# Weight splits with a priority ahead of the other work of ScalarE and VectorE, in a hybrid decoder trunk

## The chip, the core and the metric

The kernel runs on one core of a Trainium2 chip. The core has five engines that work side by side and synchronise through semaphores: TensorE (PE in the profile, its weight loads PEld), VectorE (DVE), ScalarE (ACT), GpSimd (POOL) and SyncE (SP), which here only issues DMAs. The time is the device time of one execution in microseconds (us), lower being better. Three runs of the kernel before took 806.59, 806.67 and 807.04 us; the median is 806.67.

## What is computed

Two layers of a decoder trunk on 256 tokens of width 1024, in float32. In each layer a single input projection of the normalised stream feeds three mixers; each is gated, projected, merged by a sigmoid gate, and the sum goes through one output projection into the residual:

```python
for layer in range(DEPTH):                     # 2
    h = rms_norm(x, norm_w[layer])
    proj = jnp.einsum('bsd,de->bse', h, w_in[layer])     # 1024 -> 12832
    (a_xbc, a_z, a_dt, b_q, b_k, b_v, b_z,
     c_q, c_k, c_v, c_f, c_z, gates) = jnp.split(proj, split_at, axis=-1)
    y_a = mamba2_branch(a_xbc, a_z, a_dt, ...)           # convolution, chunked scan, group norm
    y_b = sliding_window_branch(b_q, b_k, b_v, b_z, ...) # rotary, 16 heads on 4 key heads, sinks
    y_c = forgetting_attention_branch(c_q, c_k, c_v, c_f, c_z, ...)  # 16 heads, decaying bias
    ys = jnp.stack([y_a, y_b, y_c], axis=2)
    branch = jnp.einsum('bsiw,iwd->bsid', ys, w_proj[layer])
    g = jax.nn.sigmoid(gates.reshape(b, s, N_BRANCH, d) + gate_bias[layer])
    merged = jnp.sum(g * branch, axis=2)
    x = x + jnp.einsum('bsd,de->bse', merged, w_out[layer])
return rms_norm(x, final_norm_w)
```

## The kernel before

**Three products for one.** The large products keep float32 accuracy with a faster number format, fp32r. Each operand is split into a high part, which is its copy in fp32r, and a low part, which is what the copy leaves over. A product is then high by high, plus low by high, plus high by low. `split` (lines 287 to 295) makes the two parts: one copy on ACT (line 290) and one subtraction on DVE (line 291), which needs the copy. It is used for the weights, which pass through it while the kernel runs, and for a few activations.

**Weights as a stream.** All weight matrices are cut into parts of 128 rows by 1024 numbers per partition (mostly four blocks of 256 columns or two of 512), in the order in which the products use them. `load_part` (line 351 on) issues a part's DMA on SP's queue into one of 6 `raw` buffers. `feed` (lines 383 to 396) takes the next part, allocates one of 6 `hi` and one of 6 `lo` buffers, and issues its split; then it has the next parts loaded, up to 6 ahead. `feed` is called by `release` (line 403) as soon as the matmuls that use a part for the last time have been written down, so at most 4 parts (`AHEAD`) are held by the program at that point; the buffers allow 6. Key and query weights (`turned`) are split in two halves with their columns rearranged.

**Work on PE.** PE's order is the order of the program text: the last two blocks stand in `tc.manual_schedule` for PE. `ops` lists the products, each a function such as `u_conv`, `u_cq`, `u_gate` or `u_proj`. Most of them accumulate one bank of PSUM (tag `mm`, 3 banks, rotated) over 8 blocks of 128 rows. After each product `pump` lets other work of PE in, in small doses: the generators `swa_quad`, `fox_quad`, `ssd_group` and others yield estimated waiting times (the `D_...` constants), and `pump` resumes one when its time is due on an estimated clock of PE. These use the tag `mx`, 5 banks. A product is emptied from its bank by ACT (lines 486 and 487 for the sums that GpSimd's queue then adds by an accumulating DMA, line 488; line 478 with line 479 on DVE where DVE adds them).

**Softmax chains.** `attn_quad` handles four heads: PE computes the scores, DVE subtracts a mask or bias and finds the maximum (L615, L623 to L628 for the sliding window, L646 for the forgetting attention), ACT takes the exponential and its sum (L610 or L652), DVE normalises (L635 to L639 with one small step on ACT, or L655 to L658), PE transposes the result (L113) and multiplies it by the values. There are 4 such quads of each kind in a layer.

**Order on ACT and DVE.** Only the opening is ordered by hand on all engines (the block at line 1425). For the rest a scheduler fixes each engine's queue at compile time: it walks through an estimated execution, and where several instructions of an engine could start, it takes the one that stands earliest in the program text. `tc.high_priority()` places the instructions traced inside it ahead of that order. Before the change it stands around the evictions of the first branch's projection (line 1015), the last branch's merge (line 1144) with the transposes and split behind it (line 1151), the layer's last additions and its norm (line 1204), and the split of the normalised stream of the next layer (line 1254). `pin` (line 284) does the opposite: it keeps an instruction behind what its engine has been given before; the splits of the last weights ahead of the output projection are pinned (`limit`, line 398), and appear in the profile under line 285, the wrapper's.

Of the kernel before, what the change touches and what calls it, by code (L numbers as in the profile page):

```python
# [16 lines left out]
P = 128  # L17
# [33 lines left out]
def hybrid_trunk(  # L51
# [17 lines left out]
    def T(tag, shape, dtype=F32, bufs=None):  # L69
        count[0] += 1  # L70
        return sb.tile(shape, dtype, tag=tag, name=f"{tag}_{count[0]}",
                       bufs=bufs if bufs is not None else BUFS.get(tag, 1))
# [8 lines left out]
    def pmx():  # L81
        return PS("mx", 5)
# [204 lines left out]
    def split(hi, lo, src, scale=None, keep=lambda f: f):  # L287

        if scale is None:
            keep(act)(hi, src, AF.Copy)  # L290
            keep(tt)(lo, src, hi.bitcast(F32), op=ALU.subtract)  # L291
        else:
            keep(act)(hi, src, AF.Copy, scale=scale)
            keep(stt)(lo, src, scale, hi.bitcast(F32), op0=ALU.mult, op1=ALU.subtract)
# [37 lines left out]
    turned = set()  # L332
    subs = []
    ops = []
    stream = []
    state = {"load": 0, "split": 0, "held": 0, "limit": None, "pin": False}
# [27 lines left out]
    def load_to(n_):  # L364

        while state["load"] < min(n_, len(stream)):
            load_part(state["load"])
            state["load"] += 1

    def new_part():  # L370

        j = state["split"]
        i, k = stream[j]
        n = subs[i][1]
        w = pieces.setdefault(i, Piece(n))
        load_to(j + 1)
        hi, lo = (T(tag, [P, min(NK - k, w.kper), n], F32R) for tag in ("hi", "lo"))
        state["held"] += 1
        w.parts.append((hi, lo))
        state["split"] += 1  # L380
        return raws.pop(j), hi, lo

    def feed(i=-1):

        lim = state["limit"]
        while state["split"] < len(stream) and state["split"] != lim and (
                state["held"] < AHEAD or stream[state["split"]][0] <= i):
            raw, hi, lo = new_part()
            keep = pin if state["pin"] else lambda f: f
            if stream[state["split"] - 1][0] in turned:  # L390
                for c in range(2):
                    split(*(v[:, :, c * P:(c + 1) * P].rearrange("p k (h e) -> p k h e", h=4) for v in (hi, lo)),
                          raw.rearrange("p k (h c e) -> p c k h e", h=4, c=2)[:, c, :, :, :], keep=keep)
            else:
                split(hi, lo, raw, keep=keep)
            load_to(state["split"] + N_RAW)

    def limit(j, keep):

        state["limit"], state["pin"] = j, keep  # L400
        feed()

    def release(w, n):
        if n > w.released:
            state["held"] -= n - w.released
            w.released = n
            feed()

    def run_op(i, f, last):
        if i is None:  # L410
            f()
            return
        feed(i)
        w = pieces[i]
        w.last = last
        f(w)
        if last:
            release(w, len(w.parts))
# [852 lines left out]
    for y in layers:  # L1271
# [11 lines left out]
        def cols(c0, n=256):  # L1283
            return sub([(0, w[:, c0:c0 + n])], n)
# [39 lines left out]
        if l == 0:  # L1324
            v, cv0, cv1 = cols(C_BV), cols(C_CV), cols(C_CV + 256)
# [8 lines left out]
        else:  # L1334
            cv0, v = cols(C_CV, 512), cols(C_BV)
# [89 lines left out]
    with tc.manual_schedule(engines={ENG.PE, ENG.DVE, ENG.Activation, ENG.Pool}):  # L1425
# [11 lines left out]
        p = pmx()  # L1437
# [98 lines left out]
        v = T("sm", [P, 8])  # L1536
# [55 lines left out]
```

## Time and profile before

| | us |
|---|---|
| median of 3 runs | 806.67 |
| the profiled execution's own time | 806.9 |
| its span, first to last instruction | 805.1 |
| PE busy, over 5160 matmul records | 796.5 |
| DVE busy | 684.2 |
| ACT busy | 533.8 |
| GpSimd busy | 167.5 |
| DMA, mean over the span | 212 GB/s |

A line of the profile names source line, engine, operation and tiles (written `out<-in`), the shapes, how often it was seen, the busy time in us and the mean of one in ns; then how long the engine had been idle before such instructions and what ended the idle time. In a timeline a row is the start in us, the duration in us, the engine, the line and the tiles; several instructions in a row of the same kind are merged (`x3`), and the engine's idle time before them stands in brackets with what ended it. A list of waits has total, count and longest wait. PE's matmuls are pipelined and their ends modelled, so their starts say more than their ends.

### The profile page before, as it was taken

To read this page: it belongs to the slowest core of one execution; us is meant where nothing else is said; L and a number is where in the kernel's file an instruction comes from. 1 tells how busy PE (TensorE), PEld (TensorE's weight loads), DVE (VectorE), ACT (ScalarE), POOL (GpSimd) and SP (SyncE) were. 2 spreads that over 40 slices of the span, in tenths; PEclk is the share of its full clock that TensorE was granted. 3 is DMA by queue.
4 is the path that set the end of the run, shared out by engine and by line. 5 is a ranking of instruction groups with operands and counts; after the bars stand their busy time and mean duration, and the time that the engine had idled before them with its cause. 6 is when DMAs were issued, how large, how long until landed. Compare 5 with 4: busy or idle time off the path is not lost.

```text
span 805.1 us, 14840 instructions
## 1 busy us (share of the span) xinstructions
PE 796.5 (99%) x5160; PEld 711.6 (88%) x5160; DVE 684.2 (85%) x1416; ACT 533.8 (66%) x1146; POOL 167.5 (21%) x236
## 2 busy tenths in 40 slices
PE   9999999999999999999999999999999999999996
PEld 8998988888998988888998899888889989888896
DVE  6878999997998997795785799999889999969865
ACT  7776768875775885543665678687657768755452
POOL 3166213140210100033001741122311220002000
PEclk9999999999999999999999999999999999999999
DMA  9997987797765565686678987679976546576632
GB/s 316 280 259 172 253 219 200 219 290 220 198 184 167 174 187 170 219 253 205 217 251 257 239 210 217 157 217 287 285 211 196 183 143 202 156 248 210 209 106 78
DMA packets 138827, 170.43 MB, mean 212 GB/s; under 512 B 9353, under 2 KB 106465, under 8 KB 138753
## 3 DMA queue, kind: packets, MB, share of 16 engines
q1 hardware_dynamic: 114960, 140.53, 55.5%
q0 software_dynamic: 13328, 13.29, 10.3%
q10 hardware_dynamic: 10464, 15.67, 6.7%
q8 instruction: 41, 0.67, 0.3%
q14 instruction: 34, 0.27, 0.1%
HBM read 154.71 MB, written 2.16 MB: 195 GB/s over the span
## 4 chain that ended last, share of the span: by engine, by line
PE 91%; issue 3%; DMA 2%; POOL 2%; DVE 1%; ACT 1%; POOLq 0%; DVEq 0%
PE mm L109 78%; PE mx L109 9%; PE mx L113 4%; DMA L<-L 1%; DMA hb<-in_sinks_dram 1%; POOL L L488 1%; DMA L<-in_x_dram 0%; DVE L L551 0%; ACT pp L610 0%; POOL L L285 0%; POOL L L562 0%; DVE lo L291 0%; POOL sm L224 0%; POOL L L571 0%; POOL L L572 0%
## 5 line engine op out<-in xcount | busy, mean ns | idle before, releaser
L109 PE MATMUL mm<-L,hi 128*128 128x512 f32 x1056 | 354.7, 387 | 0.5 <-ACT L L487 0.3
L291 DVE TENSOR_TENSOR lo<-raw,hi 128x1024 fp32r<-128x1024 f32 (+1 forms) x276 | 313.3, 1154 | 40.9 <-ACT hi L290 36.1
L109 PE MATMUL mm<-hi,L 128*128 128x512 f32 (+2 forms) x1168 | 303.1, 349 | 0.1
L290 ACT ACTIVATE hi<-raw 128x1024 fp32r<-128x1024 f32 (+1 forms) x276 | 265.6, 982 | 50.6 <-PE mm L109 30.0
L109 PE MATMUL mm<-L,lo 128*128 128x256 f32 x1056 | 266.6, 273 | 0.0
L109 PEld LDWEIGHTS mm<-hi,L 128*128 128x128 f32 x1168 | 205.8, 190 | 23.2 <-issue 1.5
L109 PEld LDWEIGHTS mm<-L,hi 128*128 128x128 f32 x1056 | 195.1, 190 | 27.4 <-issue 3.0
L109 PEld LDWEIGHTS mm<-L,lo 128*128 128x128 f32 x1056 | 202.1, 191 | 5.3
L109 PE MATMUL mm<-lo,L 128*128 128x512 f32 (+2 forms) x584 | 201.5, 347 | 0.0
L109 PEld LDWEIGHTS mm<-lo,L 128*128 128x128 f32 x584 | 110.2, 190 | 10.7
L488 POOL DMA_DIRECT2D L<-L x68 | 60.7, 915 | 192.5 <-ACT L L487 155.2
L1074 POOL TENSOR_SCALAR_AFFINE_SELECT bias<-bias 128x128 f32<-128x128 f32 x64 | 30.8, 513 | 82.7 <-DMA bias<-cumd 82.7
L829 DVE SCALAR_TENSOR_TENSOR L<-L,vec,L 128x255 f32<-128x255 f32 (+2 forms) x96 | 46.2, 481 | 1.9 <-ACT L L826 0.4
L486 ACT ACTIVATE L<-mm 128x256 f32<-128x256 f32 x84 | 31.9, 380 | 20.0 <-PE mm L109 14.0
L652 ACT ACTIVATE pp<-pp,nm 128x128 f32<-128x128 f32 x64 | 28.2, 443 | 22.8 <-DVE nm L646 22.8
L1109 ACT ACTIVATE L<-L 128x512 f32<-128x512 f32 x24 | 15.1, 631 | 34.5 <-DVE L L1106 30.8
L610 ACT ACTIVATE pp<-pp,nm 128x128 f32<-128x128 f32 x32 | 12.6, 394 | 24.9 <-DVE nm L615 24.1
L488 POOL DMA_DIRECT2D qt<-L x16 | 14.2, 925 | 71.4 <-ACT qt L487 64.6
L1142 POOL TENSOR_TENSOR L<-L,L 128x512 f32<-128x512 f32 x8 | 12.0, 1494 | 74.0 <-DVE L L1141 74.0
L487 ACT ACTIVATE L<-mm 128x256 f32<-128x256 f32 x68 | 26.2, 386 | 1.5 <-DMA L<-L 1.5
L1106 DVE TENSOR_TENSOR L<-mm,L 128x512 f32<-128x512 f32 x22 | 15.1, 687 | 11.2 <-PE mm L109 11.2
L551 DVE TENSOR_TENSOR L<-L,cs 128x256 f32<-128x256 f32 x40 | 20.0, 536 | 4.6 <-DMA L<-L 4.6
(213 smaller groups left out, 913.7 us busy)
## 6 DMA issues: line engine op xcount, KB each, us to landing
raw<-in_w_in_dram SPq DMA_DIRECT2D x191, 512.0 KB, 5.1
raw<-in_w_proj_dram SPq DMA_DIRECT2D x48, 512.0 KB, 6.0
L<-L POOLq DMA_DIRECT2D x72, 128.0 KB, 5.4
raw<-in_w_out_dram SPq DMA_DIRECT2D x16, 512.0 KB, 5.9
bias<-cumd ACTq DMA_DIRECT2D x16, 256.0 KB, 3.4
L<-cumd ACTq DMA_DIRECT2D x8, 512.0 KB, 5.4
L<-in_gate_bias_dram ACTq DMA_DIRECT2D x12, 256.0 KB, 5.4
qt<-L POOLq DMA_DIRECT2D x16, 128.0 KB, 6.0
```

The source lines that it names most:

```text
L109: nc.tensor.matmul(o, a, b, **kw)
L113: nc.tensor.transpose(o, a, i)
L290: keep(act)(hi, src, AF.Copy)
L291: keep(tt)(lo, src, hi.bitcast(F32), op=ALU.subtract)
L486: act(halves(lo), ordered(p[:, S:2 * S]), AF.Copy)
L487: last = act(halves(out), ordered(p[:, 0:S]), AF.Copy)
L488: nc.gpsimd.dma_start(out, lo, accum_op=ALU.add)
L551: tt(m, p, cs[:, i, :], op=ALU.mult)
L652: act(pp[:, i, sl], pp[:, i, sl], AF.Exp, scale=-1.0, bias=nm[:, e:e + 1], accum_out=sums[:, e:e + 1])
L829: stt(a[:, s:S], x_[:, 0:S - s], y.vec[:, 16 * j + u:16 * j + u + 1], a[:, s:S], op0=ALU.mult, op1=ALU.add)
L1074: nc.gpsimd.affine_select(out=bias[:, i, dst], in_=bias[:, i, src], compare_op=ALU.is_ge, fill=NEG, base=0, pattern=[[-1, P]], channel_mul ...
L1106: tt(halves(g), p, halves(y.gb), op=ALU.add)
```

## The change

The call of `split` for weights in `feed`, in both its forms, is put inside `tc.high_priority()`. So the copies on ACT and the subtractions on DVE of all weight parts that are issued from there rank ahead of other instructions that could start at the same moment. What they compute, their count, the buffers, the loads, PE's order and the pinning are as before.

```diff
             raw, hi, lo = new_part()
             keep = pin if state["pin"] else lambda f: f
-            if stream[state["split"] - 1][0] in turned:
-                for c in range(2):
-                    split(*(v[:, :, c * P:(c + 1) * P].rearrange("p k (h e) -> p k h e", h=4) for v in (hi, lo)),
-                          raw.rearrange("p k (h c e) -> p c k h e", h=4, c=2)[:, c, :, :, :], keep=keep)
-            else:
-                split(hi, lo, raw, keep=keep)
+            with tc.high_priority():
+                if stream[state["split"] - 1][0] in turned:
+                    for c in range(2):
+                        split(*(v[:, :, c * P:(c + 1) * P].rearrange("p k (h e) -> p k h e", h=4) for v in (hi, lo)),
+                              raw.rearrange("p k (h c e) -> p c k h e", h=4, c=2)[:, c, :, :, :], keep=keep)
+                else:
+                    split(hi, lo, raw, keep=keep)
             load_to(state["split"] + N_RAW)
```

## The prediction

> **What bounds the kernel now.** I read the page's busy shares and its chain of waits first, then the waits of the tensor engine, then busy time by stretch, then the timelines of single softmax chains.
>
> ```profile
> PE 796.5 (99%) x5160; PEld 711.6 (88%) x5160; DVE 684.2 (85%) x1416; ACT 533.8 (66%) x1146; POOL 167.5 (21%) x236
> PEclk9999999999999999999999999999999999999999
> PE 91%; issue 3%; DMA 2%; POOL 2%; DVE 1%; ACT 1%; POOLq 0%; DVEq 0%
> ```
>
> ```profile
> PE mx L113 <- POOL ident masks.py:199: 1.5, 1, 1.5
> PE mm L109 <- ACT L L487: 0.3, 1, 0.3
> ```
>
> TensorE (PE) is busy for 796.5 of 805.1 us at full clock and makes 91% of the chain. All its listed waits add up to 1.8 us, of which 1.5 us is the first identity matrix. A busy PE can still be a slow one, so I looked at how its matmuls follow each other:
>
> ```profile
> 125.17 0.27 PE L109 MATMUL mm<-L,lo 128*128 128x256 f32 x1
> 125.28 0.38 PE L109 MATMUL mm<-L,hi 128*128 128x512 f32 x1
> 125.50 0.27 PE L109 MATMUL mm<-L,lo 128*128 128x256 f32 x1
> ```
>
> Starts are 0.11 us apart behind 256 columns and 0.22 us behind 512, so about 2,330 columns per us with nothing between them. [...]
>
> ```profile
> 80.00:120.00 40.00, 40.00 (x338) 36.45 (x337) 38.85 (x101) 28.35 (x73) 8.31 (x11) 1.00 0.88 238
> 200.00:250.00 50.00, 50.00 (x382) 45.01 (x382) 47.31 (x126) 35.80 (x85) 9.81 (x20) 1.00 0.73 206
> 780.00:805.10 25.10, 18.83 (x122) 17.20 (x120) 15.67 (x36) 9.22 (x18) 0.00 (x0) 0.95 0.18 63
> ```
>
> The columns are the stretch, its length, then busy us of PE, weight loads, VectorE (DVE), ScalarE (ACT) and GpSimd. In the attention stretches DVE is at 95 to 97% beside a PE that never rests: what is put ahead of DVE's work there pushes the rest back. PE's only long idle time is the end, 6.3 us after its last matmul.
>
> **What the change moves.** Nothing is added or removed. The 276 high parts on ACT (line 290) and the 276 low parts on DVE (line 291), less the pinned ones and the opening's, get first choice.
>
> ```profile
> L291 DVE TENSOR_TENSOR lo<-raw,hi 128x1024 fp32r<-128x1024 f32 (+1 forms) x276 | 313.3, 1154 | 40.9 <-ACT hi L290 36.1
> L290 ACT ACTIVATE hi<-raw 128x1024 fp32r<-128x1024 f32 (+1 forms) x276 | 265.6, 982 | 50.6 <-PE mm L109 30.0
>   PEld mm L109: 0.5, 2
> ```
>
> The third row is from the view of line 291: all that PE's weight loads ever waited for a low part is 0.5 us, twice. **What the change can give back** is therefore at most that 0.5 us and the 0.3 us above: weights are not late. Even where nothing competes, a split is bound by its buffer:
>
> ```profile
> 327.73 1.06 ACT L290 ACTIVATE hi<-raw 128x1024 fp32r<-128x1024 f32 x1 [0.24 <-PE mm L109]
> 329.03 1.06 ACT L290 ACTIVATE hi<-raw 128x1024 fp32r<-128x1024 f32 x1 [0.24 <-PE mm L109]
> ```
>
> Here ACT sits idle until PE lets a buffer go, every 1.30 us. So in the quiet stretches (gates and projections) nothing can move, and I cost the change there at nothing; the cover is the buffer itself. The pinned splits before the output projection keep their places as well:
>
> ```profile
> 388.68 2.35 DVE L285 TENSOR_TENSOR lo<-raw,hi 128x1024 fp32r<-128x1024 f32 x2
> ```
>
> (A pinned instruction shows line 285, the wrapper's.) The tail after PE's last matmul contains no split.
>
> **Where it costs: the softmax chains.** There the splits now stand behind the chain and run as a block when it is through. With first choice they run inside it, and each step of the chain behind them is late. PE's order is fixed, so if its transposes of the probabilities, or a bank that has to be emptied, become late, all of PE stops. I worked out three places.
>
> *First place, sliding-window chain at 119 to 125 us.*
>
> ```profile
> 123.35 0.21 ACT L635 ACTIVATE es<-es 128x4 f32<-128x4 f32 x1
> 125.00 1.07 ACT L290 ACTIVATE hi<-raw 128x1024 fp32r<-128x1024 f32 x1
> 123.21 0.69 DVE L639 TENSOR_TENSOR pp<-pp,rsum 128x512 f32<-128x512 f32 x1
> 126.61 1.22 DVE L291 TENSOR_TENSOR lo<-raw,hi 128x1024 fp32r<-128x1024 f32 x1
> 128.43 1.23 DVE L291 TENSOR_TENSOR lo<-raw,hi 128x1024 fp32r<-128x1024 f32 x1
> 124.05 0.63 PE L113 MATMUL mx<-ident,pp 128*128 128x128 f32 x4
> ```
>
> The normalisation (L639) ends at 123.90 and PE transposes at 124.05: slack 0.15 us. The next two splits of each engine would go into the chain. Two on ACT are 2.1 us; DVE's two (2.4 us) overlap with them, because the chain crosses between the engines. If they fit into an idle gap ahead of the chain they cost 0; if the engines' delays add, 4.5. I take ACT's 2.1, since ACT carries the chain's eight exponentials: 2.1 - 0.15 = **2.0** (0 to 4.4).
>
> *Second place, chain at 140 to 147 us.*
>
> ```profile
> 144.45 0.21 ACT L635 ACTIVATE es<-es 128x4 f32<-128x4 f32 x1
> 145.56 3.89 ACT L290 ACTIVATE hi<-raw 128x1024 fp32r<-128x1024 f32 x4
> 144.80 0.69 DVE L639 TENSOR_TENSOR pp<-pp,rsum 128x512 f32<-128x512 f32 x1
> 146.63 3.50 DVE L291 TENSOR_TENSOR lo<-raw,hi 128x1024 fp32r<-128x1024 f32 x3
> 147.52 0.60 PE L113 MATMUL mx<-ident,pp 128*128 128x128 f32 x4
> ```
>
> Four splits without a gap, 0.97 us each, while buffers come 1.30 us apart: a queue has formed behind the chain. Three of the four I put into it. That is 2.9 us on ACT or 3.5 on DVE; I take 3.2. Slack is 147.52 - 145.49 = 2.0, so **1.2** (0 to 4.4, when both engines' delays add).
>
> *Third place, forgetting attention with the scan, 213 to 224 us.*
>
> ```profile
> 217.69 0.41 DVE L479 TENSOR_TENSOR L<-mm,L 128x256 f32<-128x256 f32 x1
> 219.48 0.46 PE L109 MATMUL mm<-L,hi 128*128 128x512 f32 x1
> 221.14 2.96 ACT L290 ACTIVATE hi<-raw 128x1024 fp32r<-128x1024 f32 x3
> 222.29 2.35 DVE L291 TENSOR_TENSOR lo<-raw,hi 128x1024 fp32r<-128x1024 f32 x2
> ```
>
> L479 empties a bank of the three that the projections rotate through; it ends at 218.10 and PE begins a new group at 219.48, slack 1.4. Two low parts in front of it are 2.4 us: **1.0** (0 to 2.2, with three in front).
>
> **The sum.** How many such chains there are:
>
> ```profile
> L635 ACT ACTIVATE es<-es 128x4 f32<-128x4 f32 x16 | 3.1, 205 | 0.0
> L655 DVE RECIPROCAL rsum<-sums 128x4 f32<-128x4 f32 x16 | 2.8, 178 | 3.5 <-ACT pp L652 3.5
> ```
>
> Two of these per quad of heads, so 8 sliding-window and 8 forgetting quads, four of each per layer. The places shown are among the tight ones, so I take the others lower: 0.6 for a window quad, 0.3 for a forgetting one. Per layer 2.0 + 1.2 + 2 x 0.6 + 1.0 + 3 x 0.3 = 6.3, for two layers 12.6. A PE stall also gives ACT and DVE that time to catch up, so neighbouring stalls don't fully add; I keep three quarters, **9.5 us**. The profiled execution took 806.9 us (805.1 of span and 1.8 around it): 816.4 for it, and 816.2 against the median of 806.67. I predict **816**.
>
> DMA is costed at nothing: a split that runs earlier frees its raw buffer earlier, so loads start earlier, in order on the same queue.
>
> ```profile
> raw<-in_w_in_dram SPq DMA_DIRECT2D x191, 512.0 KB, 5.1
> L<-L POOLq DMA_DIRECT2D x72, 128.0 KB, 5.4
> ```
>
> What hides it is that loads already land ahead of need; where one collides with the accumulating transfers of GpSimd's queue (5.4 us to landing), a rotation comes late by part of a landing, 0 to 1 us, inside the range.
>
> **Rivals.**
>
> *Head-of-line waiting* (slower, more). The queue's order is fixed at compile time. If a split stands there at the moment at which the plan saw its buffer free, and on the chip PE frees it later, ACT waits with evictions queued behind it. For it:
>
> ```profile
> ACT hi L290 <- PE mm L109: 30.0, 43, 5.4
> ```
>
> 43 splits wait so today, 0.70 us each. Against it: PE waits for ACT only 0.3 us all the same. If each of the 16 quads gets one more such wait where slack is near zero, 16 x 0.70 = 11.2 comes on top of 9.5: 827.4 us. [...]
>
> *The slack holds* (no change). Only splits that are ready at the moment of choice jump, the scheduler picks one at a time, and PE keeps its 1.8 us of waits: 806.7, give or take 1.6. For it speaks ACT's 66%; against it a slack of 0.15 us and DVE at 95%. It is also the case in which the priority does nothing, as in the quiet stretches.
>
> *Faster.* The mechanism would be PE waiting for low parts, at the two places behind the 0.5 us, hidden elsewhere by modelled ends. It decides only if PE loses over 1.6 us there, three times what is listed; then, with all 1.8 us of listed waits gone too, the time would be 806.67 - 0.5 - 1.8 = 804.4. [...]
>
> **How the numbers follow.** A change of 0.2% (1.6 us) is about what a measurement of this kernel can tell from none. Forecast 0.69, head-of-line 0.15, no change 0.12, faster 0.04. So slower 0.84, same 0.12, faster 0.04. With no stall at any place the time is 806.7; with the upper bound at all 16 quads (8 x 4.4 + 8 x 2.2 = 52.8) 859, which needs all delays to add everywhere. I end the range at 830, a little above the head-of-line case, and begin it at 807.5, leaving out the top and the bottom end of these cases.
>
> **What would show it.** The blocks of four and three splits at 145.56 and 221.14 are gone and splits stand between the exponentials (L610, L652). PE's waits grow from 1.8 us to about 11, with entries for L639, L479 and L487, most of them in the attention stretches of both layers alike; PE busy stays near 796, the stretch from 310 to 372 us keeps its length, and the tail its 6.3 us of idle time. I am wrong in the size if PE's new waits are under 3 or over 20 us, in the mechanism if they stand at gates, projections or the layer's end, and in the sign if PE's waits shrink.

## The result and the profile after

| | before | after |
|---|---|---|
| median | 807.04 us (5 runs) | 845.24 us (5 runs) |
| lowest to highest | 806.59 to 807.49 | 844.71 to 846.99 |
| the profiled execution: span | 805.1 | 843.0 |
| PE busy | 796.5 | 807.4 |

The change makes the kernel slower: the ratio is 1.0477, with a 95% interval of 1.0465 to 1.0489. The forecast was 816. Lines of the kernel behind line 390 have a number higher by one in the profile after (L479 is now L480), and by a few more in kernels with added lines.

The busy shares and the granted clock of the page after:

```profile
PE 807.4 (96%) x5160; PEld 716.7 (85%) x5160; DVE 685.3 (81%) x1416; ACT 536.4 (64%) x1146; POOL 164.4 (20%) x236
PEclk9899999999999999999999999999999999999999
```

DVE and ACT do the same work as before. PE has no more to do either, yet is busy 10.9 us longer, and the clock row has an 8 in its second slice. What PE waited for, after (total, count, longest, in us):

```profile
PE mm L109 <- DVE L L480: 12.0, 13, 2.6
PE mm L109 <- DVE L L291: 3.7, 1, 3.7
PE mm L109 <- ACT bias L534: 3.6, 1, 3.6
PE mx L109 <- DVE L L961: 2.4, 1, 2.4
PE mm L109 <- ACT L L488: 1.9, 3, 1.6
PE mx L113 <- DVE pp L640: 1.8, 2, 1.0
```

Before, all waits of PE were 1.8 us. Six entries now hold 25.4 us. Three of them are a single long wait each, and none of those three is in a softmax chain. L480, which empties a bank of the projections, is the largest; the probabilities (L640), around which the prediction was built, hold 1.8 us.

**Where the time went.** PE's order is fixed, so the same operation of PE can be found in both traces, and how much later it starts tells what was lost up to there. From the timelines of PE, first before, then after:

```profile
22.69 0.40 PE L109 MATMUL mx<-L,ones 128*128 128x256 f32 x2
304.79 0.64 PE L109 MATMUL mx<-L,ones 128*32 128x256 f32 x8
401.18 1.04 PE L113 MATMUL mx<-ident,L 128*128 128x128 f32 x8
411.25 1.04 PE L113 MATMUL mx<-ident,L 128*128 128x128 f32 x8
699.60 0.64 PE L109 MATMUL mx<-L,ones 128*32 128x256 f32 x8
```

```profile
29.51 0.60 PE L109 MATMUL mx<-L,ones 128*128 128x256 f32 x2
322.32 0.64 PE L109 MATMUL mx<-L,ones 128*32 128x256 f32 x8
418.70 1.04 PE L113 MATMUL mx<-ident,L 128*128 128x128 f32 x8
434.17 1.04 PE L113 MATMUL mx<-ident,L 128*128 128x128 f32 x8
732.78 0.63 PE L109 MATMUL mx<-L,ones 128*32 128x256 f32 x6
```

| stretch (times of before) | delay at its end | lost in it | predicted, before the factor 3/4 |
|---|---|---|---|
| opening, to 22.7 | 6.8 | 6.8 | 0 |
| first layer's attention and scan, to 304.8 | 17.5 | 10.7 | 6.3 |
| its gates and projections, to 401.2 | 17.5 | 0.0 | 0 |
| boundary between the layers, to 411.3 | 22.9 | 5.4 | 0 |
| second layer's attention and scan, to 699.6 | 33.2 | 10.3 | 6.3 |
| second layer's group norm and the rest, to 805.1 | 37.9 | 4.7 | 0 |

**The opening.** ACT and PE after, then both before:

```profile
19.01 1.06 ACT L290 ACTIVATE hi<-raw 128x1024 fp32r<-128x1024 f32 x1 [0.29 <-DMA raw<-in_w_in_dram]
21.24 1.06 ACT L290 ACTIVATE hi<-raw 128x1024 fp32r<-128x1024 f32 x1 [1.18 <-DMA raw<-in_w_in_dram]
22.21 0.46 ACT L534 ACTIVATE bias<-mx,rs 128x256 f32<-128x256 f32 x1
22.76 1.06 ACT L290 ACTIVATE hi<-raw 128x1024 fp32r<-128x1024 f32 x1
23.72 0.46 ACT L534 ACTIVATE bias<-mm,rs 128x256 f32<-128x256 f32 x1
24.23 0.79 PE L109 MATMUL mm<-hi,L 128*128 128x256 f32 x2 [3.63 <-ACT bias L534]
```

```profile
17.24 0.45 ACT L533 ACTIVATE bias<-mx,rs 128x256 f32<-128x256 f32 x1
17.60 0.46 ACT L533 ACTIVATE bias<-mm,rs 128x256 f32<-128x256 f32 x1
20.01 0.39 PE L109 MATMUL mm<-hi,L 128*128 128x256 f32 x2
```

The last row is the product that now waits until 24.23, as it stood before. The copies that empty the banks of the first values' product ended at 18.06, so the slack was 1.9 us. Now they stand behind high parts, two of which wait for their weights to land (0.29 and 1.18 us): the splits are first in ACT's queue but their data is not there, so ACT stands, although the first eviction behind them has its last input, the scale `rs`, from 17.54 us on and begins at 22.21.

**The boundary.** DVE and PE after, then both before:

```profile
418.20 3.49 DVE L291 TENSOR_TENSOR lo<-raw,hi 128x1024 fp32r<-128x1024 f32 x3
422.21 1.22 DVE L291 TENSOR_TENSOR lo<-raw,hi 128x1024 fp32r<-128x1024 f32 x1
423.41 0.68 DVE L291 TENSOR_TENSOR L<-mx,L 128x512 fp32r<-128x512 f32 x1
425.57 0.68 DVE L291 TENSOR_TENSOR L<-mx,L 128x512 fp32r<-128x512 f32 x1
426.30 0.80 PE L109 MATMUL mm<-hi,L 128*128 128x512 f32 x1 [3.67 <-DVE L L291]
```

```profile
403.90 0.69 DVE L291 TENSOR_TENSOR L<-mx,L 128x512 fp32r<-128x512 f32 x1
404.73 0.60 PE L109 MATMUL mm<-hi,L 128*128 128x512 f32 x2
```

`L<-mx,L` is the low part of the next layer's normalised stream. PE can't go on without it, and weight low parts stand ahead of both its halves. Before, the half that PE needs first ended at 404.59, and the matmul that now waits, the second in the row at 404.73, began at 404.95: 0.4 us of slack. In VectorE's compiled queue the two halves have changed places as well, so the half that PE needs first is the one at 425.57. The split of this stream had the priority before the change too; what is new is that the weights have it as well.

**The second layer's group norm.** ACT, DVE and PE after, then DVE before:

```profile
731.56 1.04 ACT L290 ACTIVATE hi<-raw 128x1024 fp32r<-128x1024 f32 x1
732.91 1.04 ACT L290 ACTIVATE hi<-raw 128x1024 fp32r<-128x1024 f32 x1
733.85 0.40 ACT L958 ACTIVATE L<-L 128x256 f32<-128x256 f32 x1
734.17 1.22 DVE L291 TENSOR_TENSOR lo<-raw,hi 128x1024 fp32r<-128x1024 f32 x1
735.31 0.42 DVE L961 TENSOR_TENSOR L<-L,L 128x256 f32<-128x256 f32 x1
735.78 0.62 PE L109 MATMUL mx<-L,ones 128*32 128x256 f32 x2 [2.37 <-DVE L L961]
```

```profile
698.09 0.42 DVE L960 TENSOR_TENSOR L<-L,L 128x256 f32<-128x256 f32 x1
```

Before, the last sum of squares ended at 698.51 and PE began with the sums at 699.60: at least 1.1 us of slack. Now two high parts stand ahead of the last square (L958) and a low part ahead of the sum (L961), on two engines one after the other.

**Forgetting attention and scan**, the prediction's third place, 213 to 224 us before. DVE and PE after:

```profile
228.10 2.34 DVE L291 TENSOR_TENSOR lo<-raw,hi 128x1024 fp32r<-128x1024 f32 x2
230.71 1.51 DVE L887 SCALAR_TENSOR_TENSOR L<-L,acum,negtri 128x128 f32<-128x128 f32 x5
232.15 0.74 DVE L480 TENSOR_TENSOR L<-mm,L 128x256 f32<-128x256 f32 x2
232.71 0.45 PE L109 MATMUL mm<-L,hi 128*128 128x512 f32 x1 [2.48 <-DVE L L480]
```

Two low parts stand ahead of the scan's decays (L887), and the evictions (L480) behind both. In the second layer the same place costs 2.59 us.

**A sliding-window chain**, the prediction's second place (140 to 147 us before). ACT after:

```profile
154.54 0.21 ACT L636 ACTIVATE es<-es 128x4 f32<-128x4 f32 x1
155.34 1.04 ACT L290 ACTIVATE hi<-raw 128x1024 fp32r<-128x1024 f32 x1
156.59 2.94 ACT L290 ACTIVATE hi<-raw 128x1024 fp32r<-128x1024 f32 x3
```

Here the splits still stand behind the chain's last step, as before. First choice did not put them into it.

**The clock.** Busy time of PE, weight loads, DVE, ACT and POOL by stretches of 1 us after, then granted clock, DMA share and GB/s:

```profile
28.00:29.00 1.00, 1.00 (x7) 1.00 (x6) 0.00 (x0) 0.00 (x0) 0.00 (x0) 0.50 1.08 356
428.00:429.00 1.00, 1.00 (x3) 0.76 (x3) 0.81 (x3) 0.00 (x0) 0.09 (x1) 0.50 1.04 364
736.00:737.00 1.00, 1.00 (x4) 0.58 (x3) 1.00 (x3) 0.39 (x1) 0.00 (x0) 0.75 0.82 299
737.00:738.00 1.00, 1.00 (x3) 0.80 (x3) 1.00 (x2) 0.00 (x0) 0.00 (x0) 0.50 0.74 190
738.00:739.00 1.00, 1.00 (x4) 0.75 (x3) 0.13 (x1) 0.26 (x1) 0.00 (x0) 0.50 0.93 311
739.00:740.00 1.00, 1.00 (x4) 0.82 (x3) 0.17 (x1) 0.80 (x1) 0.00 (x0) 0.54 0.71 238
233.00:234.00 1.00, 1.00 (x8) 0.95 (x7) 1.00 (x3) 1.00 (x3) 0.00 (x0) 1.00 0.82 267
```

Behind each of the three long waits PE gets half its clock for 3 to 6 us of matmuls (24.2 to 29.9, 426.3 to 429.3, 736.5 to 739.9): 256 columns in fp32r take 0.21 us from start to start in place of 0.11, 512 columns 0.43 in place of 0.22. (In float32, 384 columns took 0.66 us at full clock in the trace before, two products from 218.25 to 218.91.) That loses half of each stretch, 2.9, 1.5 and 1.7 us, 6.1 together. Behind the wait of 2.48 us at 232.71 the clock stayed at 1.00 in this execution; the last section compares the traces.

The sum closes roughly: listed waits 28.7 (all entries) less 1.8 of before, plus 6.1 for the clock, is 33.0 of 37.9 us. A listed wait begins at the modelled end of the matmul before it, which is 0.16 us behind the next possible start (0.38 us of busy time against 0.22 between starts, 0.27 against 0.11, in the prediction's first timeline); the 25 waits that the kernel before did not have, at 0.16, are an estimated 4.0 us more.

### The profile page after: what moved, and what is told of

It is laid out like the page before. It is cut to its first block, busy times and chain, and to the rows that moved or that the text cites. A ratio compares the mean times of both kernels' runs of the same rounds, so it can differ in the third digit from the quotient of the medians.

```text
span 843.0 us, 14935 instructions
## 1 busy us (share of the span) xinstructions
PE 807.4 (96%) x5160; PEld 716.7 (85%) x5160; DVE 685.3 (81%) x1416; ACT 536.4 (64%) x1146; POOL 164.4 (20%) x236
## 5 line engine op out<-in xcount | busy, mean ns | idle before, releaser
L109 PE MATMUL mm<-hi,L 128*128 128x512 f32 (+2 forms) x1168 | 308.4, 353 | 7.9 <-DVE L L291 3.7
L109 PEld LDWEIGHTS mm<-hi,L 128*128 128x128 f32 x1168 | 209.4, 193 | 32.1 <-DVE L L291 4.0
L109 PE MATMUL mm<-lo,L 128*128 128x512 f32 (+2 forms) x584 | 203.7, 351 | 0.0
L109 PEld LDWEIGHTS mm<-lo,L 128*128 128x128 f32 x584 | 112.3, 193 | 11.0
L1075 POOL TENSOR_SCALAR_AFFINE_SELECT bias<-bias 128x128 f32<-128x128 f32 x64 | 25.3, 465 | 97.6 <-DMA bias<-cumd 93.5
L653 ACT ACTIVATE pp<-pp,nm 128x128 f32<-128x128 f32 x64 | 28.2, 442 | 20.1 <-DVE nm L647 20.1
L836 ACT ACTIVATE L<-L 128x256 f32<-128x256 f32 x32 | 13.4, 419 | 27.5 <-DVE L L830 27.5
L986 POOL TENSOR_TENSOR sm<-sm,mhalf 128x8 f32<-128x8 f32 x2 | 3.4, 1683 | 110.7 <-DVE sm L984 110.7
```

Of the source, the lines that this page charges most:

```text
L109: nc.tensor.matmul(o, a, b, **kw)
L653: act(pp[:, i, sl], pp[:, i, sl], AF.Exp, scale=-1.0, bias=nm[:, e:e + 1], accum_out=sums[:, e:e + 1])
L836: act(th, a, AF.Tanh)
L1075: nc.gpsimd.affine_select(out=bias[:, i, dst], in_=bias[:, i, src], compare_op=ALU.is_ge, fill=NEG, base=0, pattern=[[-1, P]], channel_mul ...
```

## The experiments

All times are medians, set against the kernel before as it ran on the same chip (806.8 to 807.2 us).

**1 and 2. Do the costs lie where the delay appears?** The priority is left out around the three long waits, or kept only there (j is the number of the weight part):

```diff
-            with tc.high_priority():
+            with (tc.high_priority() if not (j < 14 or 128 <= j < 144 or 226 <= j < 240) else nullcontext()):   # e_quiet3
+            with (tc.high_priority() if (j < 26 or 126 <= j < 144 or 226 <= j < 240) else nullcontext()):       # e_only3
```

> The change, but without the priority for the weight parts that are split around the three long stalls of PE: the first 10 parts behind the opening, 16 parts at the boundary between the layers, 14 parts at the group norm of the second layer. Theory A (the cost is local: 6.6 us in the opening, 5.2 at the boundary, 4.5 at the group norm, the rest in the two layers' attention and scan stretches): 845.2 - 6.6 - 5.2 - 4.5 = 828.9 us, within 2, and a granted clock of 1.00 behind the opening, at the boundary and at the group norm. Rival B (a split that is not served early at one place queues up and the delay comes back later): 836 us or more.

> The counterpart: the priority only for the parts around the three long stalls (opening, layer boundary, group norm), none in the attention and scan stretches or at gates and projections. Theory A (local costs that add): 807.0 + 16.3 = 823.3 us, within 2, with three waits of PE of 3.6, 3.7 and 2.4 us and nearly nothing else. Rival B (the backlog that the splits in the attention stretches leave behind is what makes those three places late): under 815 us.

Measured: 827.80 us without the three (ratio 1.0255, 1.0238 to 1.0272) and 824.61 with them alone (1.0218, 1.0203 to 1.0233). Theory A holds in both by the time. The waits of the second are 4.0, 3.0 and 2.4 us, and 2.2 us of waits for evictions (L481) just ahead of the group norm. The two costs over before, 20.9 and 17.7, add up to 38.5, against 38.2 for the whole change. The two sets of parts are not exact complements: 14 to 25, 126 and 127 have the priority in both; experiment 9, which gives it to 14 to 25 too, loses nothing. So next to nothing is caught up between places or handed on.

**3 and 4. ScalarE or VectorE?** The priority for one half of each split only (`ranked` puts a single call inside `tc.high_priority()`):

```diff
+            keep = lambda f: ranked(first_(f)) if f is act else first_(f)    # e_hi;  "if f is tt" in e_lo
```

> Priority for the high parts on ScalarE only; the low parts on VectorE stand in the text's order as before. Theory A (PE waits for VectorE behind low parts that were put ahead): only the opening's stall (6.6 us) and the waits for the evictions on ScalarE (1.9 us) come: 807.0 + 8.5 = 815.5 us, within 3. Rival B (ScalarE's order is what moves everything, VectorE only follows it): 835 us or more.

> Priority for the low parts on VectorE only; the high parts on ScalarE stand in the text's order as before. Theory A: the boundary (5.2 us), the group norm (4.5 us) and the waits for VectorE in the attention stretches (12.0 + 1.8 + 1.1 = 14.9 us) come, the opening does not: 807.0 + 24.6 = 831.6 us, within 5. Rival B (a low part can't run ahead of its high part, which keeps its place): under 815 us.

Measured: 831.56 us for the high parts (1.0303, 1.0276 to 1.0329) and 821.27 for the low parts (1.0177, 1.0159 to 1.0195). None of the four expectations holds: ScalarE's order alone costs more than VectorE's (24.6 us against 14.3), though most of the waits name VectorE. The waits of PE with the high parts alone show why:

```profile
PE mm L109 <- ACT bias L542: 3.9, 1, 3.9
PE mx L109 <- DVE L L969: 2.4, 1, 2.4
```

The group norm's wait is named after VectorE's sum (L969 here), and it is there in full with VectorE's low parts left in the text's order: the square that the sum needs is late on ScalarE. The engine that a wait names is the last link, and need not be the one whose order was changed. With the low parts alone, that wait and the opening's are absent; the boundary (2.5 us) and the two waits at the third place (2.40 and 2.25 us) are there. That the two costs come to 38.9 together is in part chance, since the two halves meet at the same places: the boundary's wait is 2.5 us with the low parts, 0.6 with the high parts and 3.7 with both.

**5. Is it the evictions that are late?** Splits keep their priority, and what empties the banks gets the same:

```diff
+        with tc.high_priority():
+            last = act(halves(out), ordered(p[:, S:2 * S]), AF.Copy)
+        finish(last)
+        with tc.high_priority():
+            tt(halves(out), ordered(p[:, 0:S]), halves(out), op=ALU.add)
```

(and likewise in `dma_sum` and `u_bv`.)

> The change, and in addition the same priority for what empties the banks of the projections: the copies on ScalarE and the additions on VectorE of the channel sums, and the copy of the values' bank. Splits and evictions then stand in the text's order among each other. Theory A (PE stands because evictions queue behind splits and behind the chain that the splits pushed back): the 12.0 us of PE waiting for the addition that empties a bank, most of the opening's 6.6 and the 1.9 us for ScalarE go; boundary and group norm stay: 845.2 - 12 - 6 - 1.5 = 825.7 us, within 4. Rival B (the delay is only handed on, and PE then waits as long for the softmax chains' transposes or the scan): 836 us or more, with new waits for the chains' results.

Measured: 829.73 us (1.028, 1.0265 to 1.0296), at the very edge of theory A's range (829.7). PE's waits for the additions:

```profile
PE mm L109 <- DVE L L483: 4.7, 7, 1.1
```

They fall from 12.0 to 4.7 us, and the two of 2.5 us are gone. The opening keeps a wait of 1.8 us for another ScalarE step. By the starts of the same operations of PE as above, the two attention stretches still lose 5.2 and 6.3 us, against 10.7 and 10.3 (they run from 25.15 to 312.46 and from 424.76 to 719.36 us in this trace). So getting the evictions out earlier gives back a little under half of the loss there. By the list of waits, what remains is mainly evictions again (the 4.7 us, and 1.3 for copies on ScalarE) and the probabilities. Rival B's handing on is not shown: the waits for the probabilities are 2.8 us in place of 1.8, but with the changed kernel's own queues (experiments 10 and 11) they are 3.0 and 2.7 too.

**6. The same priority for the evictions, but none for the splits.**

> The kernel before, with the priority for the evictions alone (the ones of e_evict) and none for the weight splits. Theory A (in the kernel before, evictions are in time, so that e_evict's 15.5 us against the changed kernel are a repair of what the splits did and no gain of its own): 806.8 us, within 1.5. Rival B (evictions ahead of the chains are worth something by themselves, or cost something): under 805 or over 809 us.

Measured: 809.19 us (1.0026, 1.0016 to 1.0036), rival B by a narrow margin: the evictions' priority costs 2 us by itself. What it gives back in experiment 5 is therefore a repair.

**7 and 8. How far may a split jump?** The priority moves it ahead by a number of places of the text in place of all the way:

```diff
-            with tc.high_priority():
+            with tc.high_priority(offset=min(40, tc.tile_snap_priority())):    # e_off40;  80 in e_off80
```

> The priority lets a split go ahead by 40 places of the text only (some 5 us of PE's work) in place of all the way to the front. Theory A (cost in proportion to how far the queues are reordered; about a quarter as many instructions change places on ScalarE): 807 + 9 = 816 us, within 4. Rival B (what counts is passing the work that PE needs next, and that stands within those 40 places): 835 us or more. Rival C (up to some distance it costs nothing): 807 to 809 us.

> The priority lets a split go ahead by 80 places of the text. With 40 places the cost was 1.4 us of 38; with 80, four fifths as many instructions of ScalarE change places as with the full priority, the opening's among them. Theory A (cost goes by the places changed): 807 + 0.8 x 38 = 837 us, within 4. Rival B (the cost is low until a split passes what PE needs within its slack of some microseconds, and 80 places are just beyond that): 815 to 828 us, with the opening's stall (6.6 us) and those of the second layer's group norm only in part.

Measured: 808.26 us for 40 places (1.0018, 1.0009 to 1.0027) and 816.41 for 80 (1.0118, 1.0099 to 1.0136), against 845.24 for the whole way. 40 places cost 1.4 us (in rival C's range, though not nothing). 80 places cost 9.6 us, a quarter of the whole (rival B). Cost does not go by how much is reordered, but by which hand-offs lose more than their slack: of ScalarE's 1146 instructions 91 stand at another place than before with 40 places, 377 with 80 and 488 with the whole way, but 98 in experiment 2, which costs 17.7 us. With 80 places the opening's wait is 1.4 us in place of 3.6, the two at the third place are 0.7 each, and the boundary and the group norm have none. A limited distance also makes waits that the whole way does not have, two of 1.1 us with 40 places and two of 1.3 and 1.4 with 80, one in each layer. They are the kind that the prediction was built on: with 40 places a low part stands ahead of the step of a sliding-window chain (L677) that masks the transposed probabilities, which ends at 113.23, and PE goes on at 113.38. (The list of waits names L782, the instruction right behind it on VectorE.)

**9. Where nothing competes.** The priority only behind the opening, behind the boundary, and in the gates and projections of both layers:

> The priority only in the stretches in which nothing competes: the first gate and keys behind the opening, the gates and projections from 300 to 410 us, the same behind the boundary, and everything behind the second group norm. Theory A (a split there is bound by its buffer, nothing can move and nothing is gained): 806.9 us, within 1.5. Rival B (there the earlier weights save PE something): 805 us or less. Rival C (costs there too): 809 us or more.

Measured: 806.73 us (0.9998, 0.9988 to 1.0008). Theory A by the time: nothing is lost there, and earlier weights gain nothing either. But it is not so that nothing moves: 57 of ScalarE's instructions stand at another place than before.

**10 to 12. The clock.** ScalarE's and VectorE's queues stay as changed (instruction by instruction in the traces of 10 and 11; in that of 12, 8 of ScalarE's stand elsewhere). PE gets transposes of the identity just before the products that wait:

```diff
+    def beside(n):
+        p = pmx()
+        for i in range(n):
+            nc.tensor.transpose(p[:, 0:P], ident, ident)
```

(and the calls, `beside(24)`, `beside(24)` and `beside(16)`, ahead of the three products, in 12 two of `beside(18)` more.)

> The changed kernel with nothing moved on ScalarE and VectorE; PE alone gets 24, 24 and 16 transposes of the identity matrix into a spare bank, 0.11 us each, just before the products that make the three long waits (opening, boundary, group norm). They give PE work during a time that it waits anyway. Theory A (about a third of the cost of a long wait is the clock that is granted afterwards): the waits end at the same time, but the clock stays at 1.00 behind them, and the three places cost their waits alone, 3.6 + 3.7 + 2.4 = 9.7 instead of 16.3 us: 838.6 us, within 1.5. Rival B (the slower matmuls behind the waits have another cause): 844 us or more, with a granted clock of 0.5 to 0.65 at the same places.

Measured: 846.53 us (1.0481, 1.0459 to 1.0503). By the number, rival B; but in its trace the clock behind the opening and the group norm is 1.00, and only at the boundary, where the transposes stood behind the waiting product, it falls (6.82 us of half clock, 423.0 to 429.9). Experiment 11 puts them ahead of it.

> As e_fill, but at the layer boundary the 24 transposes now stand before the product that has the long wait (in e_fill they stood behind it, so the wait of 4.0 us stayed whole, 6.4 us of half clock followed, and the transposes cost 2.6 us of their own). ScalarE's and VectorE's queues are those of the changed kernel. Theory A (a long wait costs itself plus the lower clock behind it): the clock stays at 1.00 at all three places, which cost 9.7 instead of 16.3 us: 838.6 us, within 2. Rival B (other waits take up what the clock gives): 843 us or more.

Measured: 841.94 us (1.0437, 1.041 to 1.0464), between the theories. The clock is 1.00 at all three places, but two other waits, at the third place of each layer, are now followed by half clock, though they kept it in the profile after. The windows of e_fill2 behind these two:

```profile
232.00:233.00 1.00, 1.00 (x5) 0.82 (x4) 1.00 (x4) 0.47 (x1) 0.00 (x0) 0.50 0.80 302
642.00:643.00 1.00, 1.00 (x4) 0.82 (x4) 1.00 (x3) 0.87 (x1) 0.00 (x0) 0.50 0.82 336
```

> As e_fill2, with 18 more transposes of the identity ahead of the two products that wait 2.3 to 2.7 us for a bank in the forgetting attention (one in each layer). In the profile of e_fill2 these two waits, and not the three filled ones, were followed by 3.4 us of half clock each, though in the profile of the changed kernel they were not. Theory A (any wait of more than some 2 us can cost the clock, in some executions and not in others): with all five filled the clock is 1.00 throughout, 838.9 us (842.2 of the profiled execution less 2 x 1.65), within 1.5, and the runs lie within 2 us of each other in place of 4. Rival B (the spread and the rest of the cost have another cause): 841 us or more, with a spread as before.

Measured: 840.01 us (1.0401, 1.0387 to 1.0416), with runs from 838.05 to 840.65. With all five waits filled the granted clock is 1.00 in each of the windows of 1 us up to 800 us. The time is within theory A's range. Against the changed kernel's 845.24 that is 5.2 us, gained by giving PE useless work. The runs spread over 2.6 us in place of e_fill2's 3.9, not the 2 that was expected; what makes the rest of the spread stays open.

## Why the prediction was right or wrong

- **PE is the bound, and nothing can be gained: right.** Experiment 9 measures 0.9998 where the priority competes with nothing.
- **Gates, projections and the tail lose nothing: right.** The stretch from 304.8 to 401.2 us has the same length in both traces, to 0.01 us. The reason given, that nothing can move there, is not quite what experiment 9 shows: splits do move, and PE doesn't feel it.
- **Slower, because work of the chains is pushed behind splits: right in direction.** But the mechanism holds at fewer places than named. In the second place the splits stayed behind the chain; the prediction took four in a row for a queue held up by the chain and moved three of them, and what they did wait for no run shows. The first place shows no wait for the probabilities either.
- **The third place was the right mechanism at the wrong size.** It was priced at 1.0 us (0 to 2.2) and cost 2.5 in one layer and 2.6 in the other. Further on in the same stretches, where it priced 0.3 a quad, there are more waits for L480 of 0.2 to 1.2 us. The prediction took one quad as tight and the rest as loose without looking at their slack. The attention stretches lost 10.7 and 10.3 us, against 6.3 each.
- **The factor of three quarters was wrong.** Costs of separate places added in full (20.9 and 17.7 us against 38.2 for the whole change, experiments 1 and 2).
- **The step that failed most: opening, boundary and group norm at nothing.** The prediction counted the opening as ordered by hand. The hand's order ends before the values' banks are emptied, and the splits issued from there have the priority. The boundary was covered with the pinned splits before the output projection, which "keep their places"; that is true of the last weights, but not of the next layer's first ones, which now stand ahead of the normalised stream's low part. The group norm was not looked at. These three cost 6.8, 5.4 and up to 4.7 us, 16.9 of 37.9. Each of their slacks was in the trace before: 1.9 us at the opening, 0.4 at the boundary and at least 1.1 at the group norm, as shown above. The prediction had itself written that waits at projections or the layer's end would prove the mechanism wrong; for these 16.9 us they do.
- **What would show it:** the tail kept its 6.3 us (PE is busy 6.7 of the last 13.0 us). PE's waits grew to 28.7 us, beyond the 20 at which the prediction called its size wrong, and PE busy did not stay at 796.
- **What lay outside all cases:** that a stall costs more than its length. The clock adds about 5 us (845.24 against 840.01 with the waits filled, experiment 12). The range ended at 830; the 859 that the prediction had worked out with all delays adding everywhere was nearer, but by luck: it added delays at softmax chains that did not come.
- **Head-of-line waiting**, a rival, was right in kind at the opening, where a split that waits 1.18 us for its data holds the eviction behind it. It was priced at the softmax chains, where it is not what the waits show.

## What to carry to other kernels

Before a class of work gets first choice of an engine, list every hand-off to the bounding engine over the whole program (evictions, norms, layer boundaries, the first products), with its slack, and count each whose slack is less than the pieces that would be put ahead, on every engine of the chain that leads to it. Where the priority can be limited in distance, 40 places cost 0.2% here and the whole way 4.8%, and neither gained anything. The costs of separate places added here (20.9 and 17.7 us against 38.2), so the places that were not examined are the error.

## What the hardware showed that was not expected

Long waits of PE were followed by half clock, but those of middle length not always. In the traces of both kernels and of experiments 1 to 5, 7, 8 and 10 to 12 together, from 10 to 800 us, the seven waits of 3.0 us and more (3.00 to 4.05) lost the clock, and the four of 1.7 to 2.2 kept it. Of the seventeen in between, eight lost it (the shortest 2.22) and nine kept it (the longest 2.95). The same wait at the group norm shows it best: with 2.37 us it lost the clock in the profile after and with 2.36 in e_hi, and with 2.37 in e_evict and 2.36 in e_only3 it kept it. So no length of wait divides the two in these traces.

The length of the half-clock stretches is far more regular. In windows of 0.2 us in the trace after the clock is 0.50 in a stretch and 1.00 beside it, with a value between only where it changes (0.72 at 425.8 us, 0.74 at 429.2). A window of 1 us with a mean clock of 0.75 thus holds 0.5 us of half clock, and the four rows at the group norm (0.75, 0.50, 0.50, 0.54) add up to (0.25 + 0.50 + 0.50 + 0.46) / 0.5 = 3.42 us. In the same way the boundary has 3.42 us (0.94, three of 0.50, 0.85) and the opening 6.82, twice as much (0.56, five of 0.50, 0.53). All fifteen stretches at these waits come to about 3.4 us (twelve) or 6.8 (three).

The stretches don't begin where the waits end: in the trace after, the clock fell at 23.1 and 425.9 us, 1.1 and 0.4 us before those two waits ended, and at 736.5 us, 0.7 us behind the third. What sets their beginning and their length no run here shows.

Kernels with such waits also vary more from run to run: 844.71 to 846.99 after, 840.53 to 844.40 in e_fill2, against 806.59 to 807.49 before. But the kernel with 80 places, in whose trace no wait is longer than the 1.5 us for the first identity matrix, varies too (815.00 to 818.10), so the clock is not shown to be the cause.
